# First stage of a two-layer encoder: the weights' low parts, the first scalings and the partial sums change engine

## Chip, core and metric

The kernel runs on one NeuronCore of a Trainium2 chip. The metric is the device time of the program in microseconds (us), the median of three runs. Engines are named as the profile names them: PE is TensorE (PEld its weight loads), DVE is VectorE, ACT is ScalarE, POOL is GpSimd, SP is SyncE, whose queue (SPq) issues all the DMA transfers here.

## Reference

Two layers over 512 tokens of width 1024: layer 0 mixes tokens with neighbourhood attention (16 heads of 64), layer 1 with a Fourier mix; each is followed by a gated feed-forward with a width-3 convolution and a residual LayerNorm. All of it is float32. Only the beginning matters for the change:

```python
cs  = jax.nn.silu(c)                                   # c: (1, 1024)
mod = jnp.einsum('bd,de->be', cs, ada_w[i]) + ada_b[i]  # (1, 6*1024)
sh1, sc1, g1, sh2, sc2, g2 = jnp.split(mod[:, None, :], 6, axis=-1)
u   = x * (1.0 + sc1) + sh1
qkv = jnp.einsum('bsd,de->bse', u, w_qkv)              # attention of layer 0
...
x = layer_norm(ALPHA * x + (1.0 + g1) * y, ln1_g[i], ln1_b[i])
```

## The kernel before

**Precision.** Each large product is made of three matmuls: an operand is split into a high part (a copy in the fast fp32r type) and a low part (the operand less its high part), and high by high, high by low and low by high are summed. For weights, `Stream.emit` does the split: ACT casts `raw` to `hi` (L211), and the engine named when the stream entry was added (`eng`, VectorE if none is named) subtracts to give `lo` (L212). `raw` has four buffers, and each of `hi` and `lo` four; a buffer of `raw` is free for the next transfer once `lo` has been made.

**First stage.** It runs over the eight chunks k of 128 channels. For a chunk, `load_chunk(k)` transfers 1 MB of modulation weights (`ada`, eight slices of 128x256: 128 shifts and 128 scales), and for even k also two chunks of x (`xt`) and the weights of two chunks for q0, k0, q1 (384 columns, `wqk0`) and for half of v (512 columns, `wv`). Then

- `cond_accumulate(k)` multiplies each slice by a column of cs and adds them up on VectorE, in two partial sums: two scalings (L367), six multiply-adds (L369, in place), and one addition of the two sums (L371). (Chunk 0 has its own `cond_first`, half of it on TensorE.)
- `cond_reduce(k)` sums over the partitions with two one-column products against ones, into the bank `red`.
- `cond_finish(k)` makes the chunk's bias and scale on VectorE (L381, L382), then u on ACT (L393), its high part on ACT (L394) and its low part `u0l` on VectorE (L395).
- `first_qk(k)` issues nine matmuls of 512 columns (q0, k0, q1) and `first_v(k)` twelve (four banks of v).

The loop places `first_qk(k)`, then `cond_reduce(k+1)` and `cond_finish(k+1)`, then for even k the splits of the next pair of weights, then `cond_accumulate(k+2)`, then `first_v(k)`. After the stage come, for seven head pairs, projections, scores, transposes of the probabilities (`transpose_probs`, L577) and the weighing of values; the bias tiles of the scores (`bm`, L518 and L522) are made on GpSimd. `gate_row` needs a modulation vector that `ada_accumulate` sums from eight more transfers; it splits it (L137, L138), sums it over partitions with four matmuls (`g`) and adds it to a broadcast row that it transfers itself (L159, L168).

**Order.** The framework's planner orders each engine's instructions ahead of time by program order and by its own estimate of when each is ready; each engine then runs its queue in that fixed order. `with after(ins):` makes every instruction traced in the block that is on the same engine as `ins` come after it in that engine's queue; instructions on other engines are not bound by it.

Of the kernel before, what the change touches and what calls it, by code (L numbers as in the profile page):

```python
# [13 lines left out]
ALU = mybir.AluOpType  # L14

P = 128
# [35 lines left out]
def tile_hybrid_encoder(ctx: ExitStack, tc: tile.TileContext, xT, x, cols_d, rows_d, ada0, ada_w, wqk0, wqk, wv,  # L52
                        wo, fnwo, up, down, rpb, mask_d, cas_seq, cas_ch, out):
    nc = tc.nc
    V, A, G, T = nc.vector, nc.scalar, nc.gpsimd, nc.tensor
# [12 lines left out]
    def bank(name, aux=False):  # L68
        if aux:
            return psum.tile([P, 512], F32, tag="aux", name=name, bufs=2)  # L70
        return psum.tile([P, 512], F32, tag="bank", name=name, bufs=6)

    def after(ins):

        return tc.issue_after(ins.ins)

    def f32(ap):
        return ap.bitcast(F32)

    def mm(o, lhsT, rhs, start, stop):  # L80
        return T.matmul(o, lhsT=lhsT, rhs=rhs, start=start, stop=stop)  # L81
# [11 lines left out]
    ones_r = const.tile([P, P], F32R, name="ones_r")  # L93
# [12 lines left out]
    cs = const.tile([P, KT], F32, name="cs")  # L106
# [55 lines left out]
    def gate_row(accs, l, v, name):  # L162

        row = bcast_row(ROW_GATE + 2 * l + (0 if v == 2 else 1), f"{name}_row")
        bs = ada_row_sums(accs[(l, v)], name)
        for h in range(2):
            r = row[:, h * 512 : (h + 1) * 512]
            V.scalar_tensor_tensor(out=r, in0=bs[h], scalar=1.0, in1=r, op0=ALU.add, op1=ALU.add)  # L168
        return row
# [50 lines left out]
    W = Stream()  # L220
# [71 lines left out]
    iqk, iv0, iv1 = {}, [], []  # L292

    iqk0 = []
    for j in range(4):
        iqk0.append(W.add(wqk0[j], [P, 2, 384], eng=G))
        iv0.append(W.add(wv[0, j], [P, 2, 512], eng=G))
    iqk[1] = [None, W.add(wqk[PAIRS + 1], [P, KT, P], eng=G)]
    iv1 = [W.add(wv[1, j], [P, 2, 512]) for j in range(4)]
    for p in range(2, PAIRS):  # L300
# [21 lines left out]
    def load_chunk(k):  # L322

        raws = []
        n = 2 if k == 0 else 4
        for h in range(2):
            raw = bigt([P, 4, 256], F32, f"ada0_{k}_{h}")
            for i in range(0, 4, n):
                nc.sync.dma_start(out=raw[:, i : i + n, :], in_=ada0[k, :, 4 * h + i : 4 * h + i + n, :])
            raws.append(raw)  # L330
        if k % 2 == 0:
            xt[k // 2] = bigt([P, 2, S], F32, f"xt{k // 2}")
            if k > 0:
                nc.sync.dma_start(out=xt[k // 2], in_=xT[k // 2])
        if k == 0:
            nc.sync.dma_start(out=xt[0][:, 0, :], in_=xT[0, :, 0, :])
            W.load(iv0[0])
            nc.sync.dma_start(out=xt[0][:, 1, :], in_=xT[0, :, 1, :])
        elif k % 2 == 0:
            W.load(iv0[k // 2])  # L340
        return raws

    accq, redq, done = {}, {}, {}
# [15 lines left out]
        redq[0] = red  # L359

    def cond_accumulate(k):
        pair = tmp.tile([P, 2, 256], F32, tag="t", name="acc0")
        acc = [pair[:, j, :] for j in range(2)]
        for i in range(KT):
            r, o = raws[k][i // 4][:, i % 4, :], acc[i % 2]
            if i < 2:
                V.tensor_scalar(out=o, in0=r, scalar1=cs[:, i : i + 1], scalar2=None, op0=ALU.mult)  # L367
            else:
                V.scalar_tensor_tensor(out=o, in0=r, scalar=cs[:, i : i + 1], in1=o, op0=ALU.mult, op1=ALU.add)  # L369
        accq[k] = acc[0]  # L370
        return V.tensor_tensor(out=acc[0], in0=acc[0], in1=acc[1], op=ALU.add)  # L371

    def cond_reduce(k):
        acc, red = accq.pop(k), bank("red", aux=True)
        for b in range(2):
            mm(red[:, b : b + 1], acc[:, b * P : (b + 1) * P], f32(ones_r[:, 0:1]), True, True)
        redq[k] = red

    def cond_finish(k):
# [31 lines left out]
    raws = [load_chunk(k) for k in range(3)]  # L411
    cond_first()
    W.emit(iqk0[0])
    with after(cond_finish(0)):
        cond_accumulate(1)
# [32 lines left out]
    def evict_split(hi, lo, b, scale=None):  # L448
        if scale is None:
            done["act"] = A.copy(out=hi, in_=b)  # L450
            done["dve"] = V.tensor_tensor(out=lo, in0=b, in1=f32(hi), op=ALU.subtract)
        else:
            A.mul(hi, b, scale)
            V.scalar_tensor_tensor(out=lo, in0=b, scalar=scale, in1=f32(hi), op0=ALU.mult, op1=ALU.subtract)
# [20 lines left out]
    def proj_qk(p):  # L475
        res = []
        for ip in range(2):
            if iqk[p][ip] is None:
                res.append(qb1)
                continue  # L480
            b = bank(f"qk{p}_{ip}", aux=True)
            wh, wl = W.get(iqk[p][ip])
            for k in range(KT):
                step = -1 if ip == 0 else 1
                uh, ul = u0[0][k // 2][:, k % 2, ::step], u0[1][k // 2][:, k % 2, ::step]
                last = mm3(b, wh[:, k, :], wl[:, k, :], uh, ul, k == 0, k == KT - 1)
            res.append(b)
        evict_qk(p, *res)
        return last

    def proj_v1():
        banks = [bank(f"v1_{kb}") for kb in range(4)]
        for j in range(4):
            vh, vl = W.get(iv1[j])
            for i in range(2):
                uh, ul = u0[0][j][:, i, :], u0[1][j][:, i, :]
                k = 2 * j + i
                for kb in range(4):
                    c = slice(kb * P, (kb + 1) * P)
                    mm3(banks[kb], uh[:, c], ul[:, c], vh[:, i, :], vl[:, i, :], k == 0, k == KT - 1)  # L500
        evict_v(1, banks)
# [65 lines left out]
    def transpose_probs(p):  # L567
        for hh in range(2):
            head = 2 * p + hh
            pt = probs.pop(head)  # L570
            ph, pl = PT[hh]
            b0, b1 = bank(f"pt{head}_0"), bank(f"pt{head}_1")
            for o, j, f, rows in ((b0[:, 64:192], 1, 0, slice(0, P)), (b0[:, 192:256], 0, 0, slice(64, P)),
                                  (b0[:, 256:384], 2, 0, slice(0, P)), (b0[:, 384:512], 1, 128, slice(0, P)),
                                  (b1[:, 0:128], 3, 0, slice(0, P)), (b1[:, 128:256], 2, 128, slice(0, P)),
                                  (b1[:, 256:320], 0, 128, slice(0, 64)), (b1[:, 320:448], 3, 128, slice(0, P))):
                T.transpose(out=o, in_=pt[rows, j, f : f + P], identity=ident[rows, rows])  # L577
            evict_split(ph[:, 64:512], pl[:, 64:512], b0[:, 64:512])
            evict_split(ph[:, 512:960], pl[:, 512:960], b1[:, 0:448])

    def weigh_values(p):
        t = bigt([P, 2, S], F32R, f"ao{p}")
        for hh in range(2):
            b = bank(f"av{p}_{hh}")
            h = (2 * p + hh) % 8
            for n, kb in enumerate((0, 3, 1, 2)):
                v = Vt[(p // 4, kb)][:, h * P : (h + 1) * P]
                o = OUT_AT[kb]
                for m, z in enumerate(PT[hh]):
                    mm(b[:, o : o + 256], v, z[:, kb * 256 : (kb + 1) * 256][:, ::-1], n == 0 and m == 0,  # L590
                       n == 3 and m == 1)

            r, r_lo = slice(64 * hh, 64 * hh + 64), slice(64 - 64 * hh, P - 64 * hh)
            bv = b.rearrange("p (h r c) -> p r h c", h=8, c=8)
            tv = t.rearrange("p t (r h c) -> p t r h c", h=8, c=8)
            d = tmp.tile([P, 8, 8, 8], F32, tag="t", name="avd")
            A.copy(out=tv[r, 0], in_=bv[r])
            V.tensor_tensor(out=d[r], in0=bv[r], in1=f32(tv[r, 0]), op=ALU.subtract)
            done["dve"] = V.tensor_tensor(out=tv[r, 1], in0=bv[r_lo], in1=d[r], op=ALU.add)
        ao[p] = t  # L600
# [23 lines left out]
    for i in range(PAIRS - 1):  # L624
        last_mm = proj_qk(i + 1)
        if i == 0:
            proj_v1()
        if i < 4:
            with after(norm):
                G.tensor_scalar(out=X[i], in0=X[i], scalar1=ALPHA, scalar2=0.0, op0=ALU.mult, op1=ALU.add)  # L630
        with after(last_mm):
            if i == 0:
                gates[(0, 2)] = gate_row(accs, 0, 2, "g1_0")
            transpose_probs(i)
        if i + 2 == PAIRS:
            with after(done["act"]), after(done["dve"]):
                W.emit(iwo[3])
        ex, rec, norm = scores(i + 1)
        weigh_values(i)
        with after(ex), after(norm):  # L640
            if i + 3 < PAIRS:
                W.emit(iqk[i + 3][1])
        if i > 0:
            with after(done["dve"]):
                ada_step(ADA[i])
# [397 lines left out]
```

## Time and profile before

| | |
|---|---|
| median of three runs | 1089.28 us (1088.37 to 1090.01) |
| profiled execution, its time | 1087.67 us |
| its span, first to last instruction | 1085.9 us |
| mean granted TensorE clock | 0.992 |
| TensorE busy with matmuls | 1056.5 us, 97% of the span |
| VectorE busy | 775.7 us, 71% |
| ScalarE busy | 433.7 us, 40% |
| GpSimd busy | 139.5 us, 13% |

The time has 1.8 us around the span. Busy shares are over the whole span; the change is in its first 75 us. In the views, a line gives engine, source line, operation, output<-inputs and shape; a bracket holds the idle time of the engine before the instruction and what ended it. An instruction's duration overlaps a little with the next, so the cost of one in a row of equal ones is read from the distance of their starts.

### The profile page before, as it was taken

The numbers are of one execution on the slowest core, as the hardware profiler recorded it, in microseconds if no ns is written. First come the engines' busy times: TensorE is split into PE (matmuls) and PEld (weight loads), VectorE is DVE, ScalarE is ACT, GpSimd is POOL, SyncE is SP. The second block draws the span as 40 slices with busy tenths as digits, with TensorE's granted clock in tenths as the row PEclk, the third lists the DMA queues.
The fourth block names the chain that finished last, engine by engine and source line by source line (L and its number), as shares of the span: only waits on it lengthen the run. The fifth ranks groups of instructions, "written<-read, shape, count | busy, mean of one in ns | idle before, by whom it ended". The sixth has DMA issues, their size and how long they took to land.

```text
span 1085.9 us, 13539 instructions
## 1 busy us (share of the span) xinstructions
PE 1056.5 (97%) x5064; PEld 875.8 (81%) x5064; DVE 775.7 (71%) x1228; ACT 433.7 (40%) x730; POOL 139.5 (13%) x169
## 2 busy tenths in 40 slices
PE   6889999999999999999999999999999999999996
PEld 4768878877988888888888788898888888888885
DVE  6777778769689988896764779868887565542356
ACT  2334656553644444434224017254444444422300
POOL 3236797610000000000000000000000000000000
PEclk9889999999999999999999999999999999999999
DMA  9638455433145655653788003404444323242401
GB/s 352 235 117 307 121 153 176 130 120 133 52 148 171 230 177 173 212 178 102 244 275 273 20 1 116 156 2 146 142 144 143 107 97 104 69 161 96 132 20 59
DMA packets 46148, 157.25 MB, mean 145 GB/s; under 512 B 5121, under 2 KB 7425, under 8 KB 46081
## 3 DMA queue, kind: packets, MB, share of 16 engines
q1 hardware_dynamic: 46080, 156.37, 43.5%
q8 instruction: 40, 0.66, 0.2%
q14 instruction: 28, 0.22, 0.1%
HBM read 154.25 MB, written 2.10 MB: 144 GB/s over the span
## 4 chain that ended last, share of the span: by engine, by line
PE 90%; DVE 4%; DMA 3%; issue 1%; ACT 1%; POOL 0%; SPq 0%; POOLq 0%; DVEq 0%; ACTq 0%
PE up L81 44%; PE dn L81 21%; PE qk L81 7%; PE fo L81 4%; PE v L81 4%; DMA ada<-in_ada_dram 2%; PE wo L81 2%; PE pt L577 2%; PE av L81 1%; PE s L81 1%; PE fy L81 1%; DVE acc L369 1%; DMA xt<-in_xT_dram 1%; PE tr L278 1%; PE fs L81 1%
## 5 line engine op out<-in xcount | busy, mean ns | idle before, releaser
L212 DVE TENSOR_TENSOR lo<-raw,hi 128x1024 fp32r<-128x1024 f32 x152 | 186.0, 1232 | 125.4 <-ACT hi L211 125.1
L211 ACT CAST hi<-raw 128x1024 fp32r<-128x1024 f32 (+1 forms) x173 | 178.4, 1043 | 243.1 <-PE up L81 129.3
L81 PE MATMUL dn<-hi,h 128*128 128x512 f32 x704 | 217.5, 389 | 0.0
L81 PEld LDWEIGHTS dn<-hi,h 128*128 128x128 f32 x704 | 132.2, 188 | 27.5
L81 PE MATMUL up<-u1h,hi 128*128 128x512 f32 (+1 forms) x384 | 142.3, 372 | 1.4 <-ACT u1h L287 1.4
L81 PE MATMUL up<-u1l,hi 128*128 128x512 f32 (+1 forms) x384 | 142.9, 373 | 0.0
L81 PE MATMUL up<-u3h,hi 128*128 128x512 f32 (+1 forms) x384 | 142.8, 372 | 0.0
L81 PE MATMUL up<-u3h,lo 128*128 128x512 f32 (+1 forms) x384 | 142.7, 372 | 0.0
L81 PE MATMUL up<-u3l,hi 128*128 128x512 f32 (+1 forms) x384 | 142.7, 372 | 0.0
L81 PE MATMUL up<-u1h,lo 128*128 128x512 f32 (+1 forms) x384 | 142.6, 372 | 0.0
L81 PE MATMUL dn<-lo,h 128*128 128x512 f32 x352 | 137.0, 389 | 0.0
L240 POOL TENSOR_TENSOR y<-ve,mhalf 128x1 f32<-128x1 f32 x16 | 10.7, 666 | 837.5 <-DVE ve L238 837.5
L124 DVE SCALAR_TENSOR_TENSOR acc<-ada,cs,acc 128x1024 f32<-128x1024 f32 x70 | 91.5, 1306 | 15.8 <-DMA ada<-in_ada_w_dram 15.3
L81 PEld LDWEIGHTS up<-u1h,hi 128*128 128x128 f32 x384 | 72.1, 188 | 14.2 <-ACT u1h L287 1.7
L81 PEld LDWEIGHTS up<-u1l,hi 128*128 128x128 f32 x384 | 72.2, 188 | 12.7 <-DVE u1l L288 0.2
L81 PEld LDWEIGHTS up<-u3h,lo 128*128 128x128 f32 x384 | 72.3, 188 | 12.5
L81 PEld LDWEIGHTS up<-u3l,hi 128*128 128x128 f32 x384 | 72.4, 188 | 12.5
L81 PEld LDWEIGHTS up<-u3h,hi 128*128 128x128 f32 x384 | 72.3, 188 | 12.4
L81 PEld LDWEIGHTS up<-u1h,lo 128*128 128x128 f32 x384 | 72.3, 188 | 12.3
L81 PEld LDWEIGHTS dn<-lo,h 128*128 128x128 f32 x352 | 66.1, 188 | 13.7
L212 POOL TENSOR_TENSOR lo<-raw,hi 128x1024 fp32r<-128x1024 f32 (+1 forms) x21 | 50.6, 2426 | 54.1 <-ACT hi L211 54.1
L686 ACT ACTIVATE gel<-conv 128x512 f32<-128x512 f32 x44 | 27.8, 631 | 63.3 <-DVE conv L683 62.9
(218 smaller groups left out, 1683.9 us busy)
## 6 DMA issues: line engine op xcount, KB each, us to landing
raw<-in_up_dram SPq DMA_DIRECT2D x88, 512.0 KB
ada<-in_ada_w_dram SPq DMA_DIRECT2D x80, 512.0 KB
raw<-in_down_dram SPq DMA_DIRECT2D x44, 512.0 KB
ada<-in_ada_dram SPq DMA_DIRECT2D x14, 512.0 KB
raw<-in_wqk_dram SPq DMA_DIRECT2D x13, 512.0 KB
raw<-in_wv_dram SPq DMA_DIRECT2D x8, 512.0 KB
raw<-in_wo_dram SPq DMA_DIRECT2D x8, 512.0 KB
raw<-in_fnwo_dram SPq DMA_DIRECT2D x8, 512.0 KB
```

The costliest lines, as they stand in the source:

```text
L81: return T.matmul(o, lhsT=lhsT, rhs=rhs, start=start, stop=stop)
L124: V.scalar_tensor_tensor(out=acc, in0=raw, scalar=cs[:, k : k + 1], in1=acc, op0=ALU.mult, op1=ALU.add)
L211: A.copy(out=hi, in_=raw)
L212: eng.tensor_tensor(out=lo, in0=raw, in1=f32(hi), op=ALU.subtract)
L240: power = G.tensor_tensor(out=y, in0=ve, in1=mhalf, op=ALU.pow)
L278: T.transpose(out=b[:, j * P : (j + 1) * P], in_=X[s][:, k * P : (k + 1) * P], identity=ident)
L369: V.scalar_tensor_tensor(out=o, in0=r, scalar=cs[:, i : i + 1], in1=o, op0=ALU.mult, op1=ALU.add)
L577: T.transpose(out=o, in_=pt[rows, j, f : f + P], identity=ident[rows, rows])
L686: A.activation(out=q, in_=t, func=AF.Square)
```

## The change

The low parts of the first stage's weights (`wqk0` and the first half of `wv`, eight splits in all) move from GpSimd to VectorE. In `cond_accumulate`, the two scalings that begin the partial sums move to ScalarE for every chunk but chunk 1. The addition of the two partial sums on VectorE goes; `cond_reduce` multiplies both with ones and lets TensorE add them in the bank, so that it has four one-column products instead of two. `gate_row` of the first gate is called after `transpose_probs(0)` instead of ahead of it.

```diff
     for j in range(4):
-        iqk0.append(W.add(wqk0[j], [P, 2, 384], eng=G))
-        iv0.append(W.add(wv[0, j], [P, 2, 512], eng=G))
+        iqk0.append(W.add(wqk0[j], [P, 2, 384]))
+        iv0.append(W.add(wv[0, j], [P, 2, 512]))
...
     def cond_accumulate(k):
         pair = tmp.tile([P, 2, 256], F32, tag="t", name="acc0")
-        acc = [pair[:, j, :] for j in range(2)]
         for i in range(KT):
-            r, o = raws[k][i // 4][:, i % 4, :], acc[i % 2]
-            if i < 2:
+            r, o = raws[k][i // 4][:, i % 4, :], pair[:, i % 2, :]
+            if i < 2 and k == 1:
                 V.tensor_scalar(out=o, in0=r, scalar1=cs[:, i : i + 1], scalar2=None, op0=ALU.mult)
+            elif i < 2:
+                A.mul(o, r, cs[:, i : i + 1])
             else:
                 V.scalar_tensor_tensor(out=o, in0=r, scalar=cs[:, i : i + 1], in1=o, op0=ALU.mult, op1=ALU.add)
-        accq[k] = acc[0]
-        return V.tensor_tensor(out=acc[0], in0=acc[0], in1=acc[1], op=ALU.add)
+        accq[k] = pair
...
     def cond_reduce(k):
-        acc, red = accq.pop(k), bank("red", aux=True)
+        pair, red = accq.pop(k), bank("red", aux=True)
         for b in range(2):
-            mm(red[:, b : b + 1], acc[:, b * P : (b + 1) * P], f32(ones_r[:, 0:1]), True, True)
+            for j in range(2):
+                mm(red[:, b : b + 1], pair[:, j, b * P : (b + 1) * P], f32(ones_r[:, 0:1]), j == 0, j == 1)
...
         with after(last_mm):
+            transpose_probs(i)
             if i == 0:
                 gates[(0, 2)] = gate_row(accs, 0, 2, "g1_0")
-            transpose_probs(i)
```

## Rows read from the trace of the kernel before

**Rows 1.** Windows: busy us (x instructions) of PE, PEld, DVE, ACT, POOL; granted clock; DMA.

```profile
0.00:75.00 75.00, 58.37 (x217) 46.35 (x218) 52.27 (x99) 24.03 (x32) 25.15 (x31) 0.91 0.62 232
...
300.00:1086.00 786.00, 776.13 (x3565) 646.40 (x3563) 550.18 (x745) 286.59 (x405) 8.44 (x12) 1.00 0.41 134
```

**Rows 2.** Waits of TensorE, whole span: us in total, times, longest us.

```profile
PE red L81 <- DVE acc L371: 7.5, 3, 3.2
```

**Rows 3.** Timeline of TensorE, first stage: start us, us, instruction, idle time before.

```profile
15.32 0.80 PE L81 MATMUL q<-u0l,hi 128*128 128x512 f32 x1 [2.26 <-DVE u0l L395]
...
24.06 0.40 PE L81 MATMUL q<-u0h,hi 128*128 128x512 f32 x1
...
33.10 0.50 PE L81 MATMUL red<-ones_r,acc 128*128 128x1 f32 x4
33.46 1.17 PE L81 MATMUL v<-hi,u0h 128*128 128x512 f32 x4
...
36.29 0.40 PE L81 MATMUL q<-u0h,hi 128*128 128x512 f32 x1
...
38.18 0.40 PE L81 MATMUL q<-u0h,lo 128*128 128x512 f32 x1
41.54 1.01 PE L81 MATMUL red<-ones_r,acc 128*128 128x1 f32 x4 [2.97 <-DVE acc L371]
42.41 2.05 PE L81 MATMUL v<-hi,u0h 128*128 128x512 f32 x4
...
47.62 0.40 PE L81 MATMUL q<-u0h,hi 128*128 128x512 f32 x1
```

**Rows 4.** Windows: the stretch behind the wait at 41.54, columns as in rows 1.

```profile
40.70:47.50 6.80, 5.96 (x16) 4.90 (x17) 4.81 (x14) 1.43 (x2) 0.04 (x1) 0.50 0.50 167
```

**Rows 5.** Timeline of VectorE and GpSimd, first stage.

```profile
12.37 2.35 POOL L212 TENSOR_TENSOR lo<-raw,hi 128x1024 fp32r<-128x1024 f32 x1 [0.26 <-ACT hi L211]
12.50 2.76 DVE L395 TENSOR_TENSOR u0l<-u,u0h 128x512 fp32r<-128x512 f32 x1
...
28.45 0.61 DVE L367 TENSOR_SCALAR acc<-ada,cs 128x256 f32<-128x256 f32 x2
28.97 1.27 DVE L369 SCALAR_TENSOR_TENSOR acc<-ada,cs,acc 128x256 f32<-128x256 f32 x3
30.16 0.68 DVE L395 TENSOR_TENSOR u0l<-xt,u0h 128x512 fp32r<-128x512 f32 x1
...
36.09 4.93 DVE L369 SCALAR_TENSOR_TENSOR acc<-ada,cs,acc 128x256 f32<-128x256 f32 x3
36.18 4.56 POOL L212 TENSOR_TENSOR lo<-raw,hi 128x768 fp32r<-128x768 f32 x2 [9.32 <-ACT hi L211]
...
59.59 1.09 DVE L367 TENSOR_SCALAR acc<-ada,cs 128x256 f32<-128x256 f32 x2
...
74.45 1.21 DVE L212 TENSOR_TENSOR lo<-raw,hi 128x1024 fp32r<-128x1024 f32 x1
```

**Rows 6.** Groups by shape: a scaled copy on ScalarE; busy us, mean ns.

```profile
L453 ACT ACTIVATE q<-q 128x384 fp32r<-128x384 f32 x2 | 1.0, 488 | 0.9 <-PE q L81 0.9
```

**Rows 7.** The bias tiles on GpSimd: ns min/median/max, first and last start us.

```profile
L522 POOL TENSOR_TENSOR bm<-bx,mask x4: 449/476/637, 58.9 to 61.0; 128x128 f32<-128x128 f32 x4
L518 POOL TENSOR_TENSOR bm<-bx,mask x2: 714/745/776, 58.3 to 59.8; 128x256 f32<-128x256 f32 x2
```

**Rows 8.** Chain that ended last: a transfer, from its issue to its landing.

```profile
25.13 9.55 DMA xt<-in_xT_dram
```

**Rows 9.** Timeline of SP's queue: the last two issues of ada, for chunk 7.

```profile
28.66 1.61 SPq L329 DMA_DIRECT2D ada<-in_ada_dram x2
```

**Rows 10.** Timeline of TensorE and GpSimd: the gate's sums, the second pair's probabilities.

```profile
105.66 0.39 PE L81 MATMUL g<-g_hi,ones_r 128*128 128x512 f32 x1
...
118.88 3.65 POOL L558 TENSOR_SCALAR p<-p,rs 128x256 f32<-128x256 f32 x8 [1.67 <-DVE rs L556]
...
124.09 2.88 PE L577 MATMUL pt<-ident,p 128*128 128x128 f32 x16
```

## The prediction

> **What bounds the kernel now.** Windows by stage come first [rows 1]. From 300 us on TensorE is busy for 776.13 of 786 us at a granted clock of 1.00: a us saved ahead of that stretch is kept, since everything behind only starts earlier. In the first 75 us TensorE is busy for 58.37 us, at a mean clock of 0.91. So the first stage is the place to look, and the list of TensorE's waits says for whom: 7.5 us in three waits for the sum of the accumulated slices (L371), the longest 3.2 [rows 2].
>
> The timeline shows what a wait costs [rows 3]. The reduction of chunk 4 could start when the nine matmuls before it end, at 38.58, and starts at 41.54, 2.97 late. The four reduction matmuls and twelve of v that follow take 6.08 us (41.54 to 47.62); the same sixteen one chunk earlier took 3.19 (33.10 to 36.29). The granted clock in that stretch is 0.50, the lower of its two levels, 1.2 instead of 2.4 GHz [rows 4]. So the wait costs 2.97 + 2.89 = 5.9 us. The same pattern stands at chunk 6, with the wait of 3.2.
>
> Why is the accumulate late? Three multiply-adds on VectorE take 1.27 us from 28.97, and 4.93 us from 36.09 [rows 5]. Beside the slow three, GpSimd makes two low parts in 4.56 us, which begin 0.09 later and end 0.28 earlier. So it is again with `u0l` of chunk 0: 2.76 us against 0.68, and GpSimd's low part of 2.35 beside it. I read this as VectorE held by GpSimd, instruction by instruction; that it waits for something else instead is rival C.
>
> **The change, part by part.** Prices of VectorE are distances between starts [rows 5]: a scaling 0.26 (two from 28.45 to 28.97), a multiply-add 0.40 (three in 1.19), a `u0l` 0.61. A low part of 1024 columns took 1.21 at 74.45; I take 1.15 for it and, by columns between that and `u0l`, 0.9 for 768.
>
> 1. *Low parts leave GpSimd.* There are four pairs of them; the last two pairs end the waits at chunks 4 and 6, the first two the wait of 2.26 for `u0l` and the remaining one of the three.
>  Chunk 4 gives 5.9 us, chunk 6 3.2 + 2.9 = 6.1. The third wait is 7.5 - 2.97 - 3.2 = 1.3. These sum to 13.3.
>  Chunk 0: unhindered, scaling, low part and `u0l` end about 12.6 instead of 15.26, and TensorE's first three matmuls occupy it until about 12.9. The wait of 2.26 goes, but the accumulate of chunk 1 (0.5 + 6 x 0.40 = 2.9) and one low part (1.15) then end between 15.5 and 16.7, where the nine matmuls end about 15.4. I take 1.5 back, between 0.9 and 2.3.
>  The matmuls of this chunk ran at the lower level (one took 0.80 at 15.32 and 0.40 at 24.06 [rows 3]). Whether TensorE, waiting less, gets 2.4 GHz sooner no row shows: from nothing to about 2.3 us (twelve of v at the higher level: 33.46 to 36.29 is 2.83, against 5.2 from 42.41 to 47.62). I take 1.0, below the middle, as only part of v would profit.
>  Gains: 13.3 + 1.5 + 1.0 = 15.8.
>
> 2. *Four products instead of two in each of seven reductions.* Two take 0.36 at the higher level (33.10 to 33.46) and 0.87 at the lower (41.54 to 42.41) [rows 3]. TensorE is what everything waits for once its waits are gone, so nothing hides it: 6 x 0.36 + 0.87 = 3.0 us lost; 6.1 if all ran at the lower level.
>
> 3. *What VectorE must now do.* For a chunk it loses two scalings and the addition of sums, 0.52 + 0.43 = 0.95 (0.43 for the addition: the slow multiply-adds end at 41.02, the reduction starts at 41.54, less 0.09 for a signal, an estimate from the 0.09 between the beginnings in rows 5), and every second chunk gains 2.05 of low parts. Between bias and scale of one chunk and the reduction of the chunk after stand, at worst, six multiply-adds (2.4), `u0l` (0.6) and both low parts (2.05), 5.05 us; with 0.09 for each signal between the engines it is 5.2. TensorE's cover is twelve of v and nine of q, 5.12 (33.46 to 38.58). That is even; since the low parts also wait for their casts I take a wait of 0.5 on each of three chunks, 1.5 us. If the low parts fit behind the multiply-adds, it is 0; if a wait pulled the clock down, 2.9 more each time. Chunks without low parts need 3.2 and are covered. A low part that ends sooner also frees its `raw` sooner, so SP's next weights start earlier; they queue behind chunk 7's slices, issued from 28.66 [rows 9], and take nothing from the stage.
>
> 4. *Scalings on ScalarE.* The nearest row is a scaled copy of 384 columns, 0.49 us [rows 6]; two of 256 are below 1.0, some 6 us for six chunks. They aren't bound by the `after`, which orders VectorE alone; they can run as soon as the slices have landed, and ScalarE is idle for 51 of the first 75 us [rows 1]. That idle time hides them, and I take nothing. Without the cover they stand behind the next u, and the multiply-adds begin 1 us late or more; put too early they hold up ScalarE (rival D).
>
> 5. *Bias tiles.* GpSimd makes them right after its low parts, for 4 x 0.476 + 2 x 0.745 = 3.4 us [rows 7]. With the low parts gone it starts as soon as the mask and table have landed, which I estimate at 43 from the last slices' issue at 28.66 to 30.3 [rows 9], a flight of 9.55 [rows 8] and the transfers queued behind; that is where chunk 6 is accumulated with its two low parts. Beside the bias tiles two scalings took 1.09 instead of 0.61 [rows 5], 0.44 lost for each us; over 3.4 us that is 1.5. I take 1.0, as part may fall where VectorE waits; bounds nothing and 3.4.
>  The Trainium skill bears on this ("SBUF — State Buffer", section "Who interferes with whom"): GpSimd and a VectorE instruction with two inputs in SBUF share one read interface, as an exclusive lock, and the later one fully blocks. The slow multiply-adds agree (4.93 beside 4.56); the scalings, which lost 0.48 beside some 1.1 us of bias tiles, agree in part. By the rule the bias tiles cost 3.4, not 1.0, and the sum below would be 7.9.
>
> 6. *The gate's sums.* Four matmuls change places with sixteen transposes on a busy TensorE: nothing. Their row's transfer moves too, in SP's queue; the update of the row stands on VectorE before the next scores. GpSimd finished those probabilities at 122.53, TensorE wanted them at 124.09 [rows 10]: 1.56 of slack before a late row costs anything. Bounds: nothing, and 1 us lost.
>
> Sum: 15.8 - 3.0 - 1.5 - 1.0 = 10.3 us. Against the profiled execution's own 1087.67 (span 1085.9 and 1.8 around it) this is 1077.4. The median lies 1.6 above that execution: 1079.0.
>
> **Rivals.**
> *A: VectorE is late enough for the clock to fall again.* The low parts and all 3.4 us of bias tiles meet at chunk 6: a wait of 0.5 + 3.4 = 3.9, more than the 2.97 after which the clock fell, so 2.9 more. Sum: 10.3 - 2.4 - 2.9 = 5.0, time 1084.3. For it: both are on VectorE's path. Against: GpSimd may be done with them before. The Trainium skill's lock of item 5 would put it here.
> *B: better than the sum.* Low parts and bias tiles fit in (2.5), chunk 0 gives its upper bounds (2.1): 14.9, time 1074.4.
> *C, slower: the slow multiply-adds aren't GpSimd's doing.* Then the accumulates stay slow, VectorE has 2.05 - 0.95 = 1.1 more on three of them, and item 2 costs 3.0: 1089.28 + 3.3 + 3.0 = 1095.6. It decides where the multiply-adds keep their 4.9 us with GpSimd idle. Against: in both cases of rows 5 VectorE ends with GpSimd, to 0.6 us.
> *D: ScalarE is held by an early scaling.* If the planner puts the scalings of a late chunk ahead of an earlier u, that u waits for a transfer: chunk 7's first half lands about 38.2 (28.66 + 9.55 [rows 8, 9]). Ahead of chunk 4's u (then about 37) it costs 1; ahead of chunk 2's (about 25) 13, more than the whole gain, and the kernel is slower, 1091 or so. It turns at a u due near 28. Against: five buffers of that tag let few sums begin early.
> *E: new waits on VectorE take all of it*, time about 1089.
>
> **How the numbers follow.** The forecast is 1079.0 with 0.58, its own range 1076.5 to 1081.5. A has 0.20, B 0.09, D 0.06 (two thirds of it slower), C 0.03, E 0.04. From 1075.0 to 1085.5 lie the forecast, nearly all of A and half of B; some 0.14 is left out above and 0.05 below. 0.2% is 2.2 us, about what a measurement of this kernel can tell from no change. Faster: 0.58 + 0.20 + 0.09 + 0.02 of D = 0.89; within: E, 0.04; slower: C and 0.04 of D, 0.07.
>
> **What would show it.** Item 1: no multiply-add of the stage above 1 us, and no granted clock of 0.50 after 30. Item 2: eight reduction matmuls in about 0.7 us. Item 3: waits for `acc` below 1 us, on every second chunk. Item 4: scaled copies on ScalarE that end before the L382 of the chunk before. Item 5: bias tiles before 50, beside slower multiply-adds. The stage's last matmul of v would end about 10 us earlier. The prediction is wrong if that end moves by 10 and the total doesn't: then a later wait, for the transfers of `ada` or the gate, has taken it back.

## The result: 13.0 us faster, and the profile after

The changed kernel takes 1075.84 us (median of four runs, 1074.50 to 1077.01), the kernel before 1088.82 beside it (four runs): a ratio of 0.9883, interval 0.9862 to 0.9903, or 13.0 us less. The forecast was 10.3 us less, 1079.0. The profiled execution, the lowest of the four, took 1074.5 us, with a span of 1072.7. Two of the ten runs of e9 below, of 1318 and 2705 us, are left out of its median as slow runs.

Where the time went is read from the last matmuls of v, which end the first stage: 73.83 + 1.07 = 74.90 before, 60.38 + 1.07 = 61.45 after. From there to the end of the span it is 1011.0 and 1011.25. So all of it, 13.45 us, comes from the first stage, and the stretch behind keeps it.

The kernel before, timeline of TensorE, the stage's last row:

```profile
73.83 1.07 PE L81 MATMUL v<-lo,u0h 128*128 128x512 f32 x4
```

After, waits of TensorE over the whole span (answers to [rows 2]):

```profile
PE red L81 <- DVE acc L371: 1.7, 3, 0.8
...
PE pt L579 <- DVE v L453: 1.0, 1, 1.0
...
PE q L81 <- DVE u0l L397: 0.2, 1, 0.2
```

The 7.5 us of waits for the accumulated slices have become 1.7, and the longest is 0.8 instead of 3.2. One wait is new, 1.0 us ahead of the transposes of the first pair's probabilities.

After, windows, columns as in [rows 1] (answers to [rows 1, 4]):

```profile
0.00:75.00 75.00, 66.50 (x318) 54.08 (x319) 51.51 (x117) 36.30 (x65) 12.90 (x29) 1.00 0.80 288
300.00:1072.00 772.00, 762.96 (x3506) 635.28 (x3504) 539.08 (x730) 279.28 (x395) 8.46 (x12) 1.00 0.42 135
40.70:47.50 6.80, 6.80 (x35) 5.69 (x34) 6.29 (x13) 4.92 (x8) 2.43 (x4) 1.00 0.79 248
```

The stretch from 40.7 that ran at a granted clock of 0.50 now runs at 1.00 with TensorE busy throughout.

After, timeline of TensorE (answers to [rows 3]; the row at 94.26 lies behind the stage):

```profile
11.02 0.79 PE L81 MATMUL q<-u0h,hi 128*128 128x512 f32 x1 [1.16 <-ACT u0h L391]
...
15.17 1.23 PE L81 MATMUL red<-ones_r,acc 128*128 128x1 f32 x8 [0.36 <-DVE acc L371]
...
19.09 0.40 PE L81 MATMUL q<-u0h,hi 128*128 128x512 f32 x1
...
25.74 0.38 PE L81 MATMUL red<-ones_r,acc 128*128 128x1 f32 x2 [0.57 <-DVE acc L371]
...
33.71 0.95 PE L81 MATMUL red<-ones_r,acc 128*128 128x1 f32 x8
34.52 1.17 PE L81 MATMUL v<-hi,u0h 128*128 128x512 f32 x4
...
49.98 0.50 PE L81 MATMUL q<-u0l,hi 128*128 128x512 f32 x1 [0.24 <-DVE u0l L397]
...
52.48 1.23 PE L81 MATMUL red<-ones_r,acc 128*128 128x1 f32 x8 [0.81 <-DVE acc L371]
...
60.38 1.07 PE L81 MATMUL v<-lo,u0h 128*128 128x512 f32 x4
...
94.26 0.87 PE L579 MATMUL pt<-ident,p 128*128 128x128 f32 x4 [0.99 <-DVE v L453]
```

The reduction of chunk 4, at 33.71, has no wait left; eight products take 0.81 (33.71 to 34.52) where four took 0.36 [rows 3]. The wait of 2.26 for `u0l` of chunk 0 is gone, and the first q matmul of chunk 1 starts at 19.09 instead of 24.06. What is left are waits of 0.36, 0.57 and 0.81 (chunks 1, 3 and 7) and 0.24.

After, timeline of VectorE, GpSimd and ScalarE (answers to [rows 5, 7]):

```profile
10.62 0.95 DVE L212 TENSOR_TENSOR lo<-raw,hi 128x768 fp32r<-128x768 f32 x1
11.48 0.69 DVE L397 TENSOR_TENSOR u0l<-u,u0h 128x512 fp32r<-128x512 f32 x1
...
34.84 2.06 DVE L371 SCALAR_TENSOR_TENSOR acc<-ada,cs,acc 128x256 f32<-128x256 f32 x5
...
36.33 0.91 ACT L369 ACTIVATE acc<-ada,cs 128x256 f32<-128x256 f32 x2
...
40.59 1.66 DVE L371 SCALAR_TENSOR_TENSOR acc<-ada,cs,acc 128x256 f32<-128x256 f32 x4
...
44.49 1.22 DVE L212 TENSOR_TENSOR lo<-raw,hi 128x1024 fp32r<-128x1024 f32 x1
...
45.07 1.22 POOL L520 TENSOR_TENSOR bm<-bx,mask 128x256 f32<-128x256 f32 x1 [36.05 <-DMA mask<-in_mask_dram]
...
46.36 2.71 DVE L371 SCALAR_TENSOR_TENSOR acc<-ada,cs,acc 128x256 f32<-128x256 f32 x4
...
48.15 1.23 POOL L524 TENSOR_TENSOR bm<-bx,mask 128x128 f32<-128x128 f32 x2
48.99 0.94 DVE L397 TENSOR_TENSOR u0l<-xt,u0h 128x512 fp32r<-128x512 f32 x1
49.34 2.80 POOL L212 TENSOR_TENSOR lo<-raw,hi 128x1024 fp32r<-128x1024 f32 x1
49.85 2.97 DVE L371 SCALAR_TENSOR_TENSOR acc<-ada,cs,acc 128x256 f32<-128x256 f32 x2
```

Beside an idle GpSimd five multiply-adds take 2.06 and four 1.66. Beside the bias tiles, from 45.07, four take 2.71 and `u0l` 0.94. Where GpSimd makes the one low part of the stage that the change leaves to it (that of `iqk[1]`, at 49.34), two take 2.97: one of them is held, as those of chunk 4 were before.

In chunk 0 an instruction with only one tensor as input (and the columns of bias and scale) was held as well: u, a TENSOR_SCALAR, took 1.85 before, beside GpSimd's low part of 1.81 that began at 10.30, and takes 0.55 after, with no low part beside it. So the wait of 2.26 for `u0l` came from two held instructions in a row, u and `u0l`. Before:

```profile
10.55 1.85 DVE L390 TENSOR_SCALAR u<-xt,mod 128x512 f32<-128x512 f32 x1
```

### The profile page after: what moved, and what is told of

The parts are those of the page before. It is cut to its first block, busy times and chain, and to the rows that moved or that the text cites. A ratio compares the mean times of both kernels' runs of the same rounds, so it can differ in the third digit from the quotient of the medians.

```text
span 1072.7 us, 13592 instructions
## 1 busy us (share of the span) xinstructions
PE 1050.7 (98%) x5092; PEld 871.7 (81%) x5092; DVE 765.6 (71%) x1217; ACT 438.8 (41%) x742; POOL 123.2 (11%) x161
## 4 chain that ended last, share of the span: by engine, by line
PE 89%; DVE 4%; DMA 2%; issue 2%; ACT 1%; SPq 1%; POOL 0%; POOLq 0%; DVEq 0%; ACTq 0%
PE up L81 45%; PE dn L81 21%; PE qk L81 6%; PE fo L81 4%; PE wo L81 2%; PE pt L579 2%; PE v L81 2%; PE av L81 1%; PE fy L81 1%; PE s L81 1%; PE q L81 1%; DVE acc L371 1%; DMA ada<-in_ada_dram 1%; PE red L81 1%; PE tr L278 1%
## 5 line engine op out<-in xcount | busy, mean ns | idle before, releaser
L212 DVE TENSOR_TENSOR lo<-raw,hi 128x1024 fp32r<-128x1024 f32 (+1 forms) x160 | 193.0, 1216 | 127.3 <-ACT hi L211 126.9
L560 POOL TENSOR_SCALAR p<-p,rs 128x256 f32<-128x256 f32 x64 | 45.3, 728 | 49.0 <-DVE rs L558 48.9
```

The source lines that it names most:

```text
L212: eng.tensor_tensor(out=lo, in0=raw, in1=f32(hi), op=ALU.subtract)
L560: norm = G.tensor_scalar(out=pt[hh][:, j, :], in0=pt[hh][:, j, :], scalar1=rs[hh][:, j : j + 1], scalar2=0.0, op0=ALU.mult, op1=ALU.add)
```

## The experiments

The first stage of each kernel, from its profiled execution: the start of the first q matmul of chunk 0, how long from there to that of chunk 1, and from there to the end of v(7) (start of the last row of v plus its 1.07). Ratios are to the kernel before, run beside it on the same chip; its medians there were 1086.95 to 1088.82. The profiled executions need between 1009.7 and 1014.9 us from the end of v(7) to the end of the span, and most of that scatter goes with the granted clock of a stretch that no edit touches (see the last section). So what an edit does to the stage is read from the last two columns, and what it does to the time from the medians.

| kernel | median us | ratio, 95% interval | q(0) at | to q(1) | to end of v(7) |
|---|---|---|---|---|---|
| before | 1088.82 | | 11.41 | 12.65 | 50.84 |
| after | 1075.84 | 0.9883 (0.9862 to 0.9903) | 11.02 | 8.07 | 42.36 |
| e1: low parts alone | 1079.18 | 0.9933 (0.9906 to 0.9959) | 11.58 | 8.18 | 46.62 |
| e8: sums alone | 1086.46 | 0.9996 (0.9973 to 1.0018) | 11.12 | 12.79 | 44.77 |
| e11: scalings alone | 1083.11 | 0.9966 (0.9950 to 0.9982) | 11.20 | 10.38 | 49.44 |
| e2: after, low parts back | 1079.95 | 0.9937 (0.9920 to 0.9955) | 11.50 | 10.59 | 42.40 |
| e3: after, scalings back | 1079.33 | 0.9933 (0.9914 to 0.9952) | 11.56 | 7.86 | 45.80 |
| e4: after, addition back | 1075.77 | 0.9896 (0.9870 to 0.9923) | 10.85 | 8.63 | 43.44 |
| e7: after, GpSimd loaded | 1087.58 | 1.0010 (0.9992 to 1.0028) | 10.93 | 8.55 | 53.76 |
| e9: after, first pair back | 1080.12 | 0.9928 (0.9910 to 0.9947) | 11.08 | 10.44 | 42.62 |
| e13: after, last three pairs back | 1076.16 | 0.9901 (0.9877 to 0.9926) | 10.91 | 8.08 | 42.74 |
| e6: after, last low part too | 1075.28 | 0.9896 (0.9867 to 0.9926) | 11.47 | 8.00 | 40.95 |
| e12: after, gate back | 1075.91 | 0.9900 (0.9872 to 0.9928) | 11.34 | 8.00 | 42.26 |
| e10: e6, gate back | 1075.87 | 0.9904 (0.9882 to 0.9927) | 11.30 | 7.84 | 41.08 |

The theory was that GpSimd's subtractions hold VectorE's multiply-adds, and that taking the low parts away gives the gain; the main rivals, that the slow multiply-adds come of something else (C), or that the other two edits are what counts.

**Is it GpSimd that holds VectorE? e7** adds the suspected cost alone: the changed kernel, in which GpSimd repeats the subtractions of the last three pairs into a tile that is still free; the low parts used stay VectorE's, and nothing reads what GpSimd writes.

```diff
+                if 2 <= i < 8:
+                    n = shape[1] * shape[2]
+                    G.tensor_tensor(out=X[3][:, :n].rearrange("p (a b) -> p a b", a=shape[1]), in0=raw, in1=f32(hi),
+                                    op=ALU.subtract)
```

> The changed kernel, with GpSimd repeating the subtraction of the last three pairs of low parts into a tile that is not used until later (the result is left unused); VectorE still makes the low parts. It adds the suspected cost alone. Theory: beside GpSimd's subtractions VectorE's multiply-adds and low parts take up to 2.5 us again, and waits for the accumulate of 2 us or more come back on chunks 4 and 6; the time is 1082 to 1088. Rival: GpSimd's work is no hindrance, the time stays at 1075 to 1077.

It took the whole gain back: 1.0010. Its waits for the sums, its clock from 30 to 60, and VectorE beside GpSimd (lines shifted by four):

```profile
PE red L81 <- DVE acc L375: 6.7, 4, 3.0
```

```profile
30.00:60.00 30.00, 27.16 (x108) 22.55 (x108) 23.85 (x38) 12.28 (x19) 14.08 (x17) 0.78 0.59 209
```

```profile
35.03 5.00 POOL L215 TENSOR_TENSOR x<-raw,hi 128x768 f32<-128x768 f32 x2 [9.23 <-ACT hi L211]
35.20 2.58 DVE L212 TENSOR_TENSOR lo<-raw,hi 128x768 fp32r<-128x768 f32 x1
37.71 2.60 DVE L375 SCALAR_TENSOR_TENSOR acc<-ada,cs,acc 128x256 f32<-128x256 f32 x1
```

GpSimd's two subtractions of 2.5 end at 37.5 and 40.0. VectorE's low part, 0.95 when free, ends at 37.78, and the multiply-add behind it, 0.48 when free, at 40.31. Each is held until one subtraction of GpSimd ends. (The added subtractions also keep `raw` and `hi` in use for longer, but the waits of TensorE that came back are for the sums.) Rival C falls.

**Is the gain that of the low parts? e1** makes the first edit alone (the low parts on VectorE, all else as before); **e2** undoes it in the changed kernel.

```diff
-        iqk0.append(W.add(wqk0[j], [P, 2, 384], eng=G))
-        iv0.append(W.add(wv[0, j], [P, 2, 512], eng=G))
+        iqk0.append(W.add(wqk0[j], [P, 2, 384]))
+        iv0.append(W.add(wv[0, j], [P, 2, 512]))
```

> The kernel before with the low parts of the first stage on VectorE, and nothing else of the change. Theory (GpSimd's subtractions hold VectorE's instructions that read two tensors in SBUF): no multiply-add above 1 us in the stage, the waits of 2.97 and 3.2 go, the stage's last matmul of v ends between 62 and 65 instead of 74.9; the time is 1077 to 1080, most of the whole change's gain. VectorE keeps 0.95 us more for a chunk than with the whole change, so waits of about 1 us stay on every second chunk. Rival (the gain comes from taking scalings and the addition off VectorE; the slow multiply-adds have another cause): VectorE only has more to do, the time is 1091 or more.

> The changed kernel with the low parts of the first stage back on GpSimd; scalings on ScalarE and sums on TensorE stay. Theory: two or three multiply-adds beside each pair of low parts take 2 us or more again; with 0.95 us less on VectorE the two long waits shrink to about 2 us each, and the granted clock falls to 0.50 behind at least one; the time is 1083 to 1088. Rival: the time stays at 1076 to 1078.

e1 fell within its range, 1079.18; its stage ended at 66.38 (11.58 + 8.18 + 46.62), later than the 62 to 65 expected: near its end TensorE waits up to 1.82 for u0h and 1.71 for u0l, and from 54 to 60 its granted clock is 0.52. e2 missed: it was to lose nearly all of the gain and kept more than half, 1079.95. The table says where: from q(1) to the end of v(7) it needs 42.40, as the changed kernel does (42.36), with all low parts on GpSimd. In the stage it loses in chunk 0 alone, 2.5 us; its profiled execution has another 0.5 from a later q(0) and 1.1 behind the stage. Its waits of TensorE, and VectorE beside a pair of low parts:

```profile
PE q L81 <- DVE u0l L397: 3.8, 2, 2.3
...
PE red L81 <- DVE acc L371: 0.4, 1, 0.4
```

```profile
32.88 0.69 DVE L397 TENSOR_TENSOR u0l<-xt,u0h 128x512 fp32r<-128x512 f32 x1
33.49 2.46 DVE L371 SCALAR_TENSOR_TENSOR acc<-ada,cs,acc 128x256 f32<-128x256 f32 x2
33.66 4.52 POOL L212 TENSOR_TENSOR lo<-raw,hi 128x768 fp32r<-128x768 f32 x2 [7.17 <-ACT hi L211]
```

GpSimd's pair still takes 4.5 us, but only two multiply-adds stand behind `u0l`, not three [rows 5]. The first has begun before GpSimd does and passes in 0.40; the second is held until the first subtraction ends (2.06 of the 2.46). Then the accumulate is done, and the second subtraction finds nothing of it to hold. Before, the third multiply-add was held by the second subtraction as well: 4.93.

**Which of the other edits does it? e8** and **e11** make them alone, with the low parts on GpSimd.

```diff
-        accq[k] = acc[0]
-        return V.tensor_tensor(out=acc[0], in0=acc[0], in1=acc[1], op=ALU.add)
+        accq[k] = acc
...
-            mm(red[:, b : b + 1], acc[:, b * P : (b + 1) * P], f32(ones_r[:, 0:1]), True, True)
+            for j in range(2):
+                mm(red[:, b : b + 1], acc[j][:, b * P : (b + 1) * P], f32(ones_r[:, 0:1]), j == 0, j == 1)
```

That was e8, which hands both partial sums to TensorE and drops the addition; e11 has the scalings on ScalarE:

```diff
-            if i < 2:
+            if i < 2 and k > 1:
+                A.mul(o, r, cs[:, i : i + 1])
+            elif i < 2:
```

> The kernel before with the two partial sums added by TensorE, and nothing else of the change. Theory: taking the addition of 0.43 off VectorE doesn't change which multiply-adds GpSimd holds; two are held, the waits of about 3 shrink to 2.5 and still pull the clock down, and the four products more cost 0.4 each; time 1087 to 1091. Rival (any 0.4 us off VectorE is enough): the long waits go, time 1080 to 1083.

> The kernel before with the two scalings of chunks 2 to 7 on ScalarE, and nothing else of the change; low parts stay on GpSimd, the sums on VectorE. Theory after the run with low parts back (the holding by GpSimd is real, but what a pair of its subtractions costs depends on how many multiply-adds are still to come when it begins; the two scalings gone, four instead of three multiply-adds are done by then and one instead of two is held): one multiply-add of 2 us beside each pair, no wait of 2 us for the accumulate in the steady part, no granted clock of 0.50 there, stage end between 64 and 68; time 1079 to 1083. Rival (the low parts alone decide): two are held as before, the waits of 3 us stay, time 1086 to 1089.

e8 has two of its three multiply-adds held, as expected, and its time can't be told from that of before (1086.46, just below its range of 1087 to 1091). Its waits for the sums were expected at about 2.5 each and are 0.73, 2.10 and 1.02, and no lower clock shows: its profiled execution kept a granted clock of 1.00 from 30 to 60 and was, at 1082.8 us, the fastest of ten, so that its 44.77 in the table isn't set against the 50.84 of before. e11's time, 1083.11, lies at the upper end of its range (1079 to 1083), and its mechanism was not the one expected: waits of over 2 us stayed (2.62 and 2.41). In e8, then in e11, VectorE and GpSimd at the third pair, and the reduction behind:

```profile
36.14 4.93 DVE L369 SCALAR_TENSOR_TENSOR acc<-ada,cs,acc 128x256 f32<-128x256 f32 x3
36.23 4.55 POOL L212 TENSOR_TENSOR lo<-raw,hi 128x768 fp32r<-128x768 f32 x2 [9.53 <-ACT hi L211]
...
41.13 0.83 PE L81 MATMUL red<-ones_r,acc 128*128 128x1 f32 x6 [2.10 <-DVE acc L369]
```

```profile
36.37 2.45 DVE L371 SCALAR_TENSOR_TENSOR acc<-ada,cs,acc 128x256 f32<-128x256 f32 x2
36.54 4.48 POOL L212 TENSOR_TENSOR lo<-raw,hi 128x768 fp32r<-128x768 f32 x2 [10.40 <-DMA raw<-in_wv_dram]
38.85 2.44 DVE L373 TENSOR_TENSOR acc<-acc 128x256 f32<-128x256 f32 x1
41.35 0.61 PE L81 MATMUL red<-ones_r,acc 128*128 128x1 f32 x4 [2.41 <-DVE acc L373]
```

e8 leaves three multiply-adds behind `u0l`, e11 two and the addition: three instructions either way, of which two are held. Only with both edits are two left, and one held. So in these profiles each edit alone leaves the 4.9 us standing, and both together end it.

**Does the place of the low parts matter anywhere but in chunk 0? e9** puts the first pair's back on GpSimd in the changed kernel, **e13** the other three and not the first.

```diff
-        iqk0.append(W.add(wqk0[j], [P, 2, 384]))
-        iv0.append(W.add(wv[0, j], [P, 2, 512]))
+        iqk0.append(W.add(wqk0[j], [P, 2, 384], eng=G if j == 0 else V))
+        iv0.append(W.add(wv[0, j], [P, 2, 512], eng=G if j == 0 else V))
```

That is e9; in e13 the two engines stand the other way round.

> The changed kernel with only the first of the four pairs of low parts (chunks 0 and 1) back on GpSimd. It separates the gain at chunk 0. Theory: the low part of chunk 0's u takes about 2.8 us again, TensorE waits over 2 us behind its third matmul, its full clock comes some us later than in the changed kernel (there by 14.2), and the matmuls of chunk 1 start near 23 to 24 instead of 19.1; the time is about 1080 to 1081. Rival (the clock rises early for another reason): only the wait comes back, chunk 1 starts near 21, the time is 1077 to 1078.

> The changed kernel with the low parts of the last three pairs on GpSimd again; those of the first pair stay on VectorE. Theory, with the scalings and the addition gone from VectorE only two multiply-adds follow u0l, so one is held for about 2.05 us by each pair and TensorE's cover hides it: from the first q matmul of chunk 0 to that of chunk 1 8.0 us as in the changed kernel, from there to the end of v(7) 42.4 as in both the changed kernel and the one with all low parts back; time 1076 to 1078. Rival, the low parts on GpSimd cost what their undoing cost as a whole (4.1 us): 1079.5 to 1080.5, with waits of 1 us or more for the accumulated sums at chunks 2, 4 or 6.

By the median e9 loses as much as putting all four pairs back does (1080.12 and 1079.95), as the theory had it; its q(1) at 21.52 is what the rival expected (near 21, against 23 to 24). So of the 5.4 us between its profiled execution and the changed kernel's only 2.7 lie in the stage (it ends at 64.14 instead of 61.45), and the other 2.7 behind it, among the scatter. e13 loses nothing that can be told (1076.16), although its wait at chunk 7 is 1.50 instead of 0.81. In e13 the held multiply-add and its reduction look like this:

```profile
30.73 2.45 DVE L371 SCALAR_TENSOR_TENSOR acc<-ada,cs,acc 128x256 f32<-128x256 f32 x2
30.91 4.52 POOL L212 TENSOR_TENSOR lo<-raw,hi 128x768 fp32r<-128x768 f32 x2 [7.17 <-ACT hi L211]
...
33.14 0.95 PE L81 MATMUL red<-ones_r,acc 128*128 128x1 f32 x8
```

The accumulate ends at 33.18, TensorE reaches the reduction at 33.14, and no wait is shown. In e9 chunk 0 has its old wait:

```profile
14.99 0.79 PE L81 MATMUL q<-u0l,hi 128*128 128x512 f32 x1 [2.26 <-DVE u0l L397]
...
17.29 0.63 PE L81 MATMUL q<-u0h,lo 128*128 128x512 f32 x1
...
21.52 0.40 PE L81 MATMUL q<-u0h,hi 128*128 128x512 f32 x1
```

**What are the scalings and the sums worth at the end? e3** and **e4** undo one each in the changed kernel.

```diff
-            if i < 2 and k == 1:
+            if i < 2:
...
-            elif i < 2:
-                A.mul(o, r, cs[:, i : i + 1])
```

That is e3, with all scalings on VectorE; e4, with the addition on VectorE and two products:

```diff
+        V.tensor_tensor(out=pair[:, 0, :], in0=pair[:, 0, :], in1=pair[:, 1, :], op=ALU.add)
...
-            for j in range(2):
-                mm(red[:, b : b + 1], pair[:, j, b * P : (b + 1) * P], f32(ones_r[:, 0:1]), j == 0, j == 1)
+            mm(red[:, b : b + 1], pair[:, 0, b * P : (b + 1) * P], f32(ones_r[:, 0:1]), True, True)
```

> The changed kernel with all scalings on VectorE again; low parts stay on VectorE, the sums on TensorE. VectorE has 0.52 more in front of each accumulate. Theory: chunks without low parts cover it (they need 3.7 of some 5.6 with the longer reductions), chunks with them are 0.5 later: three waits grow by 0.5, the stage ends at 62 to 63.5, the time is 1076.5 to 1078.5. Rival: scalings early on ScalarE held up u, and their going back gives time: the stage ends before 61.4.

> The changed kernel with the two partial sums added on VectorE again and two products in a reduction; low parts stay on VectorE, scalings on ScalarE. Theory (item 2: TensorE is what all waits for, and eight reduction matmuls take 0.81 where four take 0.36): seven reductions give 0.45 each back, 3.1 us; the addition of 0.43 makes the accumulate late by less than 0.5 on every second chunk; the stage ends 1 to 2.5 us earlier, at 59 to 60.5, the time is 1073 to 1075.5. Rival: TensorE waits for every accumulate as long as it saves or longer, the stage ends at 61.5 to 64.

e3 lost more than expected, 3.5 us (1079.33): its accumulates are late again (waits of 1.09 and 0.47 at chunk 7, and 0.55, 0.34 and 0.33 for u0h). At chunk 7 three multiply-adds take 3.84, from 51.16, beside GpSimd's low part of `iqk[1]` at 51.47, so that a third instruction behind `u0l` is dear there once more. Behind those waits the granted clock falls, to 0.61 from 55.75 to 60.18; four matmuls of v, 1.08 at the higher level, take

```profile
56.91 1.91 PE L81 MATMUL v<-hi,u0l 128*128 128x512 f32 x4
```

e4 missed: two products fewer were to gain 1 to 3 us and gained nothing (1075.77), since with the addition on VectorE stand waits of 1.02, 0.31 and 0.34 for u0h and one of 1.93 for the sums, the last beside the same low part on GpSimd (49.69) and followed by a granted clock of 0.66 from 54 to 59. Its stage ends at 62.92, where its rival had it (61.5 to 64). The waits:

```profile
PE red L81 <- DVE acc L373: 1.9, 1, 1.9
PE q L81 <- ACT u0h L396: 1.7, 3, 1.0
```

**What do the bias tiles and the last low part on GpSimd cost? e6** moves that last low part to VectorE too.

```diff
-    iqk[1] = [None, W.add(wqk[PAIRS + 1], [P, KT, P], eng=G)]
+    iqk[1] = [None, W.add(wqk[PAIRS + 1], [P, KT, P])]
```

> The changed kernel with one more low part moved from GpSimd to VectorE, that of the weights for k of pair 1 (L298). In the changed kernel it runs on GpSimd from 49.34 to 52.14 beside the last two multiply-adds of chunk 7 (2.97 us), just ahead of the stage's longest wait for the accumulate, 0.81. Theory: that wait, and the one of 0.24 before it, go; the two multiply-adds take about 1; the stage ends about 1 us earlier, at 60.4; the time is 0.5 to 1.5 us less, below what it can tell. Rival (the bias tiles made that wait, as the prediction's item 5 had it): wait and stage end stay.

The wait of 0.81 at chunk 7 went, and the stage ended 1.0 earlier, at 60.42; in the medians it can't be told (1075.28). The two multiply-adds that had taken 2.97 beside the low part:

```profile
46.62 2.71 DVE L371 SCALAR_TENSOR_TENSOR acc<-ada,cs,acc 128x256 f32<-128x256 f32 x4
...
50.11 0.87 DVE L371 SCALAR_TENSOR_TENSOR acc<-ada,cs,acc 128x256 f32<-128x256 f32 x2
```

The four beside the bias tiles still take 2.71, and the wait of 0.24 for `u0l` behind them is all that this costs TensorE; it was expected to go in e6, and one of 0.25 stayed.

**And the gate? e12** puts its row sums back ahead of the transposes; **e10** does so in e6.

```diff
+            if i == 0:
+                gates[(0, 2)] = gate_row(accs, 0, 2, "g1_0")
             transpose_probs(i)
-            if i == 0:
-                gates[(0, 2)] = gate_row(accs, 0, 2, "g1_0")
```

> The changed kernel with the gate's row sums placed ahead of the first pair's transposes again, and nothing else. Theory, the place of the gate makes the transposes wait: the wait of 0.99 us of TensorE for the low part v (L453 on VectorE) ahead of the transposes at 94.26 goes, the first stage is unchanged (its last matmul of v ends near 61.5), and the time is 1074 to 1076. Rival, that wait comes of something else (the low part of iqk[1] on GpSimd beside VectorE): it stays, at 0.4 to 1.0, and the time is that of the changed kernel, 1075.8.

> As the run before, and the gate's row sums ahead of the transposes again. In the changed kernel TensorE waits 0.99 in those transposes for a low part of v (L453), where before four matmuls of the gate, 0.93 us, stood ahead. Theory: the wait in the transposes goes to 0.1 or less, and from the end of the stage to the end of the program takes about 1 us less than in the run before. Together the version is 1 to 2.5 us below the changed kernel, near 1074. Rival: the gate's own sums come late there, TensorE waits as long for them, nothing is won.

In both the wait of 0.99 ahead of the transposes is gone and one of 0.4 (TensorE for `ptl`, ahead of av) stands in its place; the times are those of the kernels that they came from (1075.91 and 1075.84; 1075.87 and 1075.28). So the 1 to 2.5 us that e10 was to gain against the changed kernel did not come. e6, with the gate moved, has no wait there either, so the place of the gate alone doesn't make it.

## Why the prediction was right, and where it was not

The time was within the stated range (1075.0 to 1085.5), 0.7 below the forecast's own (1076.5 to 1081.5), and the sign right. That the sum came so close is luck in part: its 13.3 is the price of waits that the three edits end together, but it was booked on the first edit alone, and the other two were booked as a cost and as nothing. Set beside the table, the forecast's sum splits well. Behind chunk 0 it said 13.3 - 6 x 0.36 - 1.5 - 1.0 = 8.6; measured 50.84 - 42.36 = 8.5. In chunk 0 it said 1.5 + 1.0 - 0.87 = 1.6; measured 12.65 - 8.07 = 4.6, and 0.4 more since q(0) began earlier. So the miss lies in chunk 0; behind it the sum was right and its attribution wrong. These are single profiles: the 50.84 holds two falls of the clock that another execution may not have, as e8's 44.77 shows with held multiply-adds and waits of 3.9 for the sums. The medians agree: the low parts alone gain 8.9 us (1088.04 before, beside it, less 1079.18), the other two edits alone 8.1 (1088.04 less 1079.95), all of them 13.0.

1. *Low parts.* The mechanism (GpSimd holds VectorE, instruction by instruction) is shown by e7. The step that failed is "the last two pairs end the waits at chunks 4 and 6" as something that the first edit alone has to pay for: e2 and e13 end them with those low parts on GpSimd, since the scalings and the addition left only two instructions to hold. The low parts alone gain 50.84 - 46.62 = 4.2 us behind chunk 0, the other two edits 50.84 - 42.40 = 8.4, all three 8.5. The sign "no multiply-add of the stage above 1 us" failed at chunk 7, where two take 2.97 beside the low part that stayed on GpSimd. In chunk 0 the low part is worth 10.44 - 8.07 = 2.4 (e9 against after), where 1.5 was taken from a range of 0.9 to 2.3. That TensorE reaches its higher level sooner was put at 1.0, between 0 and 2.3: the rest of chunk 0 came to 12.65 - 10.44 = 2.2. That part is not the low part's, as e9 has it with the low part on GpSimd; what brings it stays open.
2. *Four products.* 0.81 against 0.36 is 0.45 for each of seven, 3.1 us, as forecast (3.0). But priced as a loss only, it hid what the edit gives: with the addition back (e4) VectorE is late by as much, and the time is the same.
3. *VectorE's extra work.* Waits of 0.36, 0.57, 0.81 and 0.24, 2.0 us in all, against 1.5 and 1.0 with the bias tiles. They are small, as said, but the 0.81 is not VectorE's load: it is the low part of `iqk[1]`, which the forecast had not looked for on GpSimd (e6).
4. *Scalings on ScalarE.* They run when ScalarE is free, 0.91 for two, without holding a u: rival D falls. "Nothing" was right as a cost and wrong as a worth: undone alone (e3) they cost 3.5 us, part of it by the fall of the clock in its profile.
5. *Bias tiles.* They began at 45.07 (estimate 43) and cost VectorE 2.71 - 1.66 + 0.94 - 0.69 = 1.3 us, inside the bounds, but TensorE only 0.24. The rule of the Trainium skill ("SBUF — State Buffer", "Who interferes with whom") agrees with the low parts, where the held instruction ends with GpSimd's to within 0.3 us (e2, e7); by it the bias tiles would have cost 3.4, and here VectorE lost 1.3 of the 4.3 us from 45.07 to 49.38. Rival A didn't come: the clock stayed at 1.00 through the stage.
6. *The gate.* A wait of 0.99 appeared where the bound said at most 1, but not for the reason priced: it is for a low part of v that VectorE makes (L453), not for a late row. Undoing the move (e12) changed the time by less than can be told.

Rival B's time, 1074.4, is nearer to the median than the forecast is, but its reasons hold only in part: chunk 0 gave its upper bounds, and the 2.5 us of waits did not vanish (2.0 are left). E falls with the result.

No kernel tried beats the changed one by more than the measurement can tell. e13 shows that it could do with less: the scalings, the sums and the first pair's low part carry the gain.

## What to carry to other kernels

When a second engine holds the one that matters, count the instructions that stand behind its start: each transfer of work away from there counts only when it leaves too few to be held, so two edits that do nothing or little alone can end the wait together. A forecast that gives a wait's whole price to the first edit and books the others as costs may have the right sum and still name the wrong cause; undo each edit, and make each alone, before the gain is credited. A wait that has gone at one chunk is worth looking for at the last place where GpSimd still makes such a tile.

## What was not expected of the hardware

TensorE gets to its higher level at different times in starts that look alike. With the 2.26 us wait for `u0l` in place, the q matmul at 17.29 in e9 still takes 0.63 and the one at 21.52 takes 0.40; before, the one at 15.32 takes 0.80 and the first short one of q comes at 24.06 [rows 3]. The granted clock reads 1.00 in both of these stretches of e9, so the level is read from the matmuls' own lengths. Chunk 0 needed 10.4 to 10.6 us in e2, e9 and e11 and 12.65 to 12.8 in before and e8, all with that wait. The first three have the scalings on ScalarE and the other two don't, but with one profile of each this is a pattern and no cause.

A wait of 2 to 3 us is not always followed by the lower level. Before, one of 2.97 was [rows 3, 4]; in the profiled execution of e8 one of 2.10 was not. A shorter one can be: in e4 one of 1.93 was, in e3 1.09 and 0.47 close together.

The same waits differ from profile to profile. Near 260 us, far behind the edits, TensorE waits about 1.05 and 1.45 us for `u1h` in all fourteen profiles. In six the granted clock stays at 1.00 behind them, in eight it falls. After, then e12, columns as in [rows 1]:

```profile
255.00:280.00 25.00, 22.49 (x173) 21.06 (x172) 17.70 (x45) 17.66 (x50) 1.65 (x3) 1.00 0.07 22
255.00:280.00 25.00, 22.49 (x163) 21.19 (x162) 17.21 (x45) 16.57 (x49) 1.65 (x3) 0.93 0.07 22
```

The six, the kernels before and after among them, need 1009.7 to 1011.3 us from the end of v(7) to the end of the span, the eight 1011.7 to 1014.9. So a profile can be 1 to 3 us longer behind the stage though no edit touches the stretch in which the clock falls.

The ten executions of e8 spread from 1082.8 to 1092.4, the 23 of the kernel before beside it from 1083.4 to 1092.6, the four of the changed one from 1074.5 to 1077.0. One profile of a kernel with such waits shows one case of several.
